# A weight request moved ahead of a small shift in SyncE's queue, and two subtractions moved from GpSimd to VectorE, in a two-layer decoder trunk

## The chip, the cores and the metric

The kernel runs on one core of a Trainium2 chip. The metric is the device time of one execution in microseconds, from which a median over runs is taken. Five engines work side by side, each through its own list of instructions in order: TensorE (PE in the rows, its weight loads PEld), VectorE (DVE), ScalarE (ACT), GpSimd (POOL) and SyncE (SP), which here asks for all DMA transfers.

## What is computed

Two layers over 1024 positions of width 1024: a Mamba-2 mixer, then stick-breaking attention over 16 heads of 64, each followed by a gated per-layer embedding. The change lies in the second layer:

```python
def stick_breaking_mixer(h, k, v, norm_g, w_in, q_g, w_out):
    qg = rmsnorm(h, norm_g) @ w_in
    gate = qg[..., SB_WIDTH:]
    q = rmsnorm(qg[..., :SB_WIDTH].reshape(bsz, s, SB_HEADS, SB_HEAD_DIM), q_g)
    q = (q * (1.0 / math.sqrt(SB_HEAD_DIM))).transpose(0, 2, 1, 3)
    for blk in range(s // SB_BLOCK):
        z = jnp.einsum('bhtd,bhsd->bhts', q[:, :, q0:kend], k[:, :, :kend])
        log_keep = jnp.where(strict, jax.nn.log_sigmoid(-z), 0.0)
        suffix = lax.cumsum(log_keep, axis=3, reverse=True) - log_keep
        weights = jnp.where(strict, jnp.exp(jax.nn.log_sigmoid(z) + suffix), 0.0)
        outs.append(jnp.einsum('bhts,bhsd->bhtd', weights, v[:, :, :kend]))
    return (o * jax.nn.silu(gate)) @ w_out
```

K and V come from the same normalized stream through `w_kv`.

## The kernel before

**Two-part numbers.** Every matrix is split into a high and a low part (`hilo`, L103 to L110): ScalarE writes the high part (L106), then GpSimd or VectorE subtracts it from the raw tile and writes the low part (L108 without a gain, L110 with one, always on VectorE). A product takes three matmuls, high by high, high by low and low by high.

**Pairs and steps.** Attention (`attention`) goes through 8 pairs of heads. A pair has 4 steps, p = 3, 2, 1, 0, each for 256 positions: `project` computes K, Q and V of two blocks (L55), `gate` (in steps p = 1 and 0) half of the pair's gate, `values` shifts V by one row through DMAs and subtracts (L851 to L863), `norm` the rms of K and Q. Work of two earlier steps is mixed in: `flip` transposes K and Q (L883) and splits them into `kst`, `qh` (L894, L895, ScalarE) and `ql` (L898, VectorE); `scores` (L914, L915 on TensorE, a sigmoid L916, a scan L918 on VectorE); `turn` transposes weights and splits them into `wh` (L939, ScalarE) and `wl` (L940, VectorE); `product` multiplies them with V (L948). I call the passage from the last step of one pair to the first of the next a pair change; there are 7.

**The pair's weights.** A pair needs 4 chunks of 512 KB. `Pairs.load` takes one: a DMA into one of three raw tiles (L760, pool `rawp`), then 4 high parts (L106, `g0h`) and 4 low parts (L110, `g0l`). `LOADS` says in which steps p a chunk of the next pair is asked for in the program's text; what is left is taken by `pairs.all` at the start of the pair. Six chunks have room, so four of every pair change are converted while the last gate of the old pair runs and frees their tiles: two of the pair that begins and, after them, two of the pair after it.

**The output weights.** `B2.weights` loads s_out in 8 chunks (L1095, `hh`/`hl`); `CHUNKS` says in which step the first four are asked for. The last four are loaded in step 31, the low parts on GpSimd. `B2.fill` (L1122) multiplies the first two row blocks of the output with them, mixed into the two last rounds of attention; its left-hand sides are split by `B2.ahead` into tiles that are free by then (`V`, `kq`, `vr`, `kst`).

**What sets the order.** TensorE's order is written by hand (`step`). On the other engines and in SyncE's queue a scheduler places the instructions when the program is built, by the order of the text and by estimated times; at run time each engine and each queue takes them strictly in that order, and a waiting one holds all behind it. V's shift has one buffer `vs`: a step's first shift (L853) can only be asked for when GpSimd is done with the one before (L863). In the first step of a pair L853 reads a row of zeros (`vs<-keep`).

Of the kernel before, what the change touches and what calls it, by code (L numbers as in the profile page):

```python
# [28 lines left out]
PLE = 256  # L29
EPS = 1e-6  # L30
ACT_HEADS = (0, 1)
LOADS = (2, 1)
SSB = 1
NEX = 5
EARLY = 3
# [3 lines left out]
GATE7 = {2: 1, 1: 0}  # L39
FLIP = 0.58  # L40
FILL = {32: 7, 33: 6}
CHUNKS = {30: (0, 1, 2, 3)}


def split3(nc, out, pairs):
# [740 lines left out]
def attention(k, A, rawp, hT, oTd, dbg, b2, pairs):  # L786
# [6 lines left out]
    with ExitStack() as ctx:  # L793
# [71 lines left out]
        def norm(st, p):  # L865
            kq = st.pop("kq")
            sq = wk.tile([P, 512], F32, name="sg", bufs=1)
            nc.scalar.activation(sq, kq.rearrange("p b m c -> p (b m c)"), AF.Square)
            n = 8
            ss = sm.tile([P, n], F32, name="kss")  # L870
            nc.vector.reduce_sum(ss, sq.rearrange("p (g d) -> p g d", d=64), axis=AX.X)
            y = k.rstd(sm, ss, n, 64, EPS, "kr")
            x = kq.rearrange("p b m (h d) -> p (b m h) d", d=64)
            nc.vector.tensor_tensor(x, x, y.unsqueeze(2).broadcast_to([P, n, 64]), op=ALU.mult)
            st["kn", p] = kq
# [127 lines left out]
        def step(i):  # L1003
# [34 lines left out]
            if i < n:  # L1038
                if p in LOADS:
                    pairs.step(hp + 1)  # L1040
                values(sts[hp], p)
                norm(sts[hp], p)
                if i in CHUNKS:
                    b2.weights(CHUNKS[i])
                if i == n - 1:
# [19 lines left out]
class B2:  # L1065
# [21 lines left out]
    def weights(self, kks):  # L1087
        k = self.k
        for kk in kks:
            half, i = 1 - kk // 4, kk % 4  # L1090
            if i == 0:
                self.big = [self.hp.tile([P, KT, 512], F32R, name=f"{n}{half}") for n in ("hh", "hl")]
            hi, lo = self.big
            raw = self.rawp.tile([P, 1024], F32, name="raw")
            k.nc.sync.dma_start(raw, self.A["s_out"][kk * P:(kk + 1) * P, :])  # L1095
            sl = slice(2 * i, 2 * i + 2)
            k.hilo(hi[:, sl], lo[:, sl], raw.rearrange("p (n c) -> p n c", n=2))
            self.W[kk] = [(hi[:, 2 * i + n], lo[:, 2 * i + n]) for n in range(2)]

    def ahead(self, t, h, raw, parts):  # L1100
# [190 lines left out]
```

## Time and profile before

| | |
|---|---|
| median of 3 runs | 1876.53 us (1875.95 to 1879.9) |
| the profiled execution | 1882.81 us, span of its instructions 1881.1 us |
| granted TensorE clock, mean over the span | 0.973 |
| TensorE busy | 1737.1 us, 92% |
| VectorE busy | 1177.3 us, 63% |
| ScalarE busy | 901.4 us, 48% |
| GpSimd busy | 412.6 us, 22% |

The profiled execution took 6.3 us more than the median. Busy shares are means over the span; attention runs from about 920 to 1690 us. The granted clock is 1.00 at 2.4 GHz and 0.5 at 1.2 GHz, the two levels that occur.

### The profile page before, as it was taken

Reading aid. Unit: us, or ns where it says so; the run is one execution under the profiler, and the core shown is the slowest. Engines: PE = TensorE matmul, PEld = TensorE weight load, DVE = VectorE, ACT = ScalarE, POOL = GpSimd, SP = SyncE. Lnnn points to the kernel's source line nnn. Section 1 sums busy time; section 2 is a strip of 40 time slices with the busy share of each in tenths; the row PEclk is TensorE's granted clock in tenths of the full one; section 3 lists DMA queues with packets and bytes.
Section 4 is the critical chain, followed back from the end, with each engine's and each line's share of the span. In section 5 each row is a group of like instructions: output and inputs, shape, how many; then the busy total and the mean of one; then the engine's idle time right before and its main releaser. Section 6 shows DMA issues by size and latency. Waiting matters only on the chain.

```text
span 1881.1 us, 25474 instructions
## 1 busy us (share of the span) xinstructions
PE 1737.1 (92%) x9170; PEld 1470.6 (78%) x9170; DVE 1177.3 (63%) x2394; ACT 901.4 (48%) x1976; POOL 412.6 (22%) x454
## 2 busy tenths in 40 slices
PE   7999999999999999999998979888888898689999
PEld 5768877877877877888887968787787888577887
DVE  6686387287278464345668776767676777575332
ACT  6567357358356241134455555555545455453211
POOL 0235534534534122100011101010101013311110
PEclk9999999999999999999998999898989999899999
DMA  4223223223213653322201011010101011223110
GB/s 151 73 71 96 80 72 96 74 68 102 78 63 118 219 175 106 130 95 76 90 19 53 20 48 40 29 53 16 53 16 53 28 30 57 75 90 125 41 51 34
DMA packets 96399, 139.43 MB, mean 74 GB/s; under 512 B 18161, under 2 KB 66641, under 8 KB 96273
## 3 DMA queue, kind: packets, MB, share of 16 engines
q1 hardware_dynamic: 96272, 137.80, 22.7%
q8 instruction: 72, 1.18, 0.3%
q14 instruction: 55, 0.44, 0.1%
HBM read 108.77 MB, written 24.77 MB: 71 GB/s over the span
## 4 chain that ended last, share of the span: by engine, by line
PE 69%; DVE 13%; ACT 8%; DMA 5%; issue 2%; POOL 2%; SPq 0%; DVEq 0%; POOLq 0%; ACTq 0%
PE mm L48 35%; PE mm L55 12%; PE mm L1122 4%; PE oq L948 3%; PE pq L48 2%; DMA vs<-vr 2%; DVE pt L918 2%; DVE v L236 2%; PE intra L411 2%; PE z L915 1%; PE tr L930 1%; PE inter L406 1%; ACT qh L895 1%; PE z L914 1%; ACT qh L894 1%
## 5 line engine op out<-in xcount | busy, mean ns | idle before, releaser
L48 PE MATMUL mm<-ul,wh 128*128 128x512 f32 (+1 forms) x648 | 254.0, 392 | 0.0
L48 PE MATMUL mm<-uh,wl 128*128 128x512 f32 (+1 forms) x648 | 252.5, 390 | 0.0
L48 PE MATMUL mm<-uh,wh 128*128 128x512 f32 (+1 forms) x648 | 252.4, 389 | 0.1
L918 DVE TENSOR_TENSOR_SCAN pt<-pt,keep 128x128 f32<-128x128 f32 (+7 forms) x128 | 173.1, 1357 | 19.0 <-ACT pt L916 17.6
L55 PE MATMUL mm<-g0l,hh 128*128 128x384 f32 x512 | 184.4, 360 | 0.0
L55 PE MATMUL mm<-g0h,hl 128*128 128x384 f32 x512 | 183.5, 358 | 0.0
L55 PE MATMUL mm<-g0h,hh 128*128 128x384 f32 x512 | 181.4, 354 | 0.0
L236 DVE SCALAR_TENSOR_TENSOR v<-u,convh,v 128x512 f32<-128x512 f32 x144 | 128.7, 898 | 55.1 <-ACT v L234 52.6
L939 ACT CAST wh<-tr 128x512 fp32r<-128x512 f32 (+1 forms) x160 | 85.4, 545 | 155.5 <-PE tr L933 147.9
L857 POOL TENSOR_TENSOR vs<-vs,vr 128x256 f32<-128x256 f32 x32 | 24.8, 775 | 598.1 <-DMA vs<-vr 316.1
L940 DVE TENSOR_TENSOR wl<-tr,wh 128x512 fp32r<-128x512 f32 (+1 forms) x160 | 100.7, 634 | 84.2 <-ACT wh L939 83.4
L48 PEld LDWEIGHTS mm<-ul,wh 128*128 128x128 f32 x648 | 121.7, 188 | 26.3 <-issue 2.3
L48 PEld LDWEIGHTS mm<-uh,wl 128*128 128x128 f32 x648 | 121.8, 188 | 25.5 <-issue 1.9
L48 PEld LDWEIGHTS mm<-uh,wh 128*128 128x128 f32 x648 | 121.7, 188 | 25.5 <-issue 1.1
L108 POOL TENSOR_TENSOR wl<-raw,wh 128x1024 fp32r<-128x1024 f32 x39 | 95.2, 2442 | 156.8 <-ACT wh L106 156.8
L916 ACT ACTIVATE pt<-z 128x320 f32<-128x320 f32 (+3 forms) x192 | 94.0, 490 | 67.4 <-PE z L915 66.2
L948 PE MATMUL oq<-wh,V 128*128 128x256 f32 x320 | 65.2, 287 | 46.2 <-issue 34.5
L948 PEld LDWEIGHTS oq<-wh,V 128*128 128x128 f32 x320 | 61.1, 201 | 54.4 <-issue 36.4
L55 PEld LDWEIGHTS mm<-g0l,hh 128*128 128x128 f32 x512 | 101.5, 198 | 2.2
L55 PEld LDWEIGHTS mm<-g0h,hl 128*128 128x128 f32 x512 | 101.1, 198 | 1.6
L55 PEld LDWEIGHTS mm<-g0h,hh 128*128 128x128 f32 x512 | 100.8, 197 | 1.2
L576 DVE SCALAR_TENSOR_TENSOR acc<-mm,rg,acc 128x512 f32<-128x512 f32 x64 | 47.8, 749 | 84.4 <-PE mm L48 83.6
(367 smaller groups left out, 4324.7 us busy)
## 6 DMA issues: line engine op xcount, KB each, us to landing
raw<-in_w_in SPq DMA_DIRECT2D x40, 512.0 KB
ex<-acd SPq DMA_DIRECT2D x64, 256.0 KB
raw<-in_w_b SPq DMA_DIRECT2D x32, 512.0 KB
raw<-in_m_out SPq DMA_DIRECT2D x16, 512.0 KB
raw<-in_gate SPq DMA_DIRECT2D x16, 512.0 KB
graw<-gT SPq DMA_DIRECT2D x30, 256.0 KB
gT<-zs SPq DMA_DIRECT2D x28, 256.0 KB
acc<-in_x SPq DMA_DIRECT2D x8, 512.0 KB
```

Source lines behind the costliest of these rows:

```text
L48: nc.tensor.matmul(out, lhsT=a, rhs=b, start=(i == 0), stop=(i == n - 1))
L55: nc.tensor.matmul(out, lhsT=a, rhs=b, start=(i == 0), stop=(i == n - 1))
L108: (eng or nc.gpsimd).tensor_tensor(lo, raw, hi.bitcast(F32), op=ALU.subtract)
L236: nc.vector.scalar_tensor_tensor(vv, u[:, 3 - j:3 - j + 512], w(j), vv, op0=ALU.mult, op1=ALU.add)
L411: nc.tensor.matmul(aq[hp * 64:hp * 64 + 64, jp * 256 + i * P:jp * 256 + (i + 1) * P], lhsT=xdts[2 * qt + i][:, (2 * j + hp) * 64:(2 * j + ...
L576: nc.vector.scalar_tensor_tensor(acc[:, sl], ps, k.rg[:, g, t:t + 1], acc[:, sl], op0=ALU.mult, op1=ALU.add)
L916: nc.scalar.activation(pt[:, ko:ko + n], z[:, :n], AF.Sigmoid, scale=-1.0)
L918: nc.vector.tensor_tensor_scan(pt[:, :N], pt[:, :N], keep[:, :N], 1.0, op0=ALU.mult, op1=ALU.max)
L939: nc.scalar.copy(wh[:, :c], tq[:, :c])
L940: nc.vector.tensor_tensor(wl[:, :c], tq[:, :c], wh[:, :c].bitcast(F32), op=ALU.subtract)
L948: nc.tensor.matmul(out[:, :w], lhsT=st["V"][j // 2][:, j % 2, h * P:(h + 1) * P], rhs=rhs, start=(j0 == 2 * p and i == 0), stop=(j0 == NT ...
L1122: nc.tensor.matmul(pss[n], lhsT=a, rhs=b, start=(q == 0 and i == 0), stop=(q == 1 and i == 11))
```

## The change

Three tables and one argument. `LOADS` now asks for a chunk of the next pair in each of the four steps, so nothing is left for `pairs.all`; `CHUNKS` asks for the first two s_out chunks in step 29, not 30; and the low parts of s_out chunks 5 and 7 are computed on VectorE.

```diff
-LOADS = (2, 1)
+LOADS = (3, 2, 1, 0)
...
-CHUNKS = {30: (0, 1, 2, 3)}
+CHUNKS = {29: (0, 1), 30: (2, 3)}
...
-            k.hilo(hi[:, sl], lo[:, sl], raw.rearrange("p (n c) -> p n c", n=2))
+            k.hilo(hi[:, sl], lo[:, sl], raw.rearrange("p (n c) -> p n c", n=2), eng=k.nc.vector if kk in (5, 7) else None)
```

What that does to the order, at the three places that matter. SyncE's queue at a pair change, before (L851 is the large shift of V, 127 rows, L853 and L852 are one-row shifts, L856 copies a row, L760 is a chunk of weights):

```order
L851 DMA vs<-vr 127x256
L856 DMA v_9882<-vr 128x1x1
L853 DMA vs<-keep 1x16x8
L760 DMA raw<-in_w_b 128x1024 x4
L852 DMA vs<-vr 1x16x8
```

and the same place now:

```order
L851 DMA vs<-vr 127x256
L856 DMA v_9910<-vr 128x1x1
L760 DMA raw<-in_w_b 128x1024
L853 DMA vs<-keep 1x16x8
L760 DMA raw<-in_w_b 128x1024 x3
L852 DMA vs<-vr 1x16x8
```

One chunk has moved ahead of the shift of zeros. This is so at five pair changes, from pair 1 to 2 up to pair 5 to 6; at the one from pair 6 to 7 the chunk is one of s_out. At the one from pair 0 to 1 a chunk stood ahead of L853 before already, and still does.

ScalarE at the same pair change, before:

```order
L894 CAST qh<-tr 64x256
L895 CAST qh<-tr 64x256
L829 COPY kq<-mm 128x256
L830 COPY vr<-mm 128x128
L959 COPY of<-oq 64x256
L106 ACTIVATE g0h<-raw,kvn 128x256
L916 ACTIVATE pt<-z 128x320
L106 ACTIVATE g0h<-raw,sn 128x256
```

and now:

```order
L894 CAST qh<-tr 64x256
L106 ACTIVATE g0h<-raw,kvn 128x256
L106 ACTIVATE g0h<-raw,sn 128x256
L895 CAST qh<-tr 64x256
L829 COPY kq<-mm 128x256
L830 COPY vr<-mm 128x128
L959 COPY of<-oq 64x256
L916 ACTIVATE pt<-z 128x320
```

Two conversions of weights have moved ahead of the last `qh` copy and of the copies of K, Q and V. This is so at six pair changes, from pair 1 to 2 up to pair 6 to 7. On VectorE the fourth low part (L110) of the first chunk has moved ahead of a 640 wide scan there.

GpSimd in the last steps of attention, as a piece of the difference (`hl` are low parts of s_out, chunk 4 above, 5 to 7 below in the old order; `V<-raw` is the low part of the left-hand side that the first `fill` needs):

```order
 L863 TENSOR_TENSOR V<-vs,V 128x128 x2
+L108 TENSOR_TENSOR V<-raw,V 128x512
 L108 TENSOR_TENSOR hl_15604<-raw,hh_15603 128x1024
-L108 TENSOR_TENSOR V<-raw,V 128x512
-L108 TENSOR_TENSOR hl_15604<-raw,hh_15603 128x1024 x2
 L108 TENSOR_TENSOR kst<-raw,kst 128x896
```

Chunk 5's low part no longer stands ahead of `V<-raw`, and chunk 7's no longer ahead of `kst`. On VectorE they now stand inside the chain of small operations of the last `norm`, and between two `wl`. TensorE's order is the same.

## Rows read from the trace of the kernel before

**Rows 1.** The page, part 4: the chain that ended last, by engine.

```profile
PE 69%; DVE 13%; ACT 8%; DMA 5%; issue 2%; POOL 2%; SPq 0%; DVEq 0%; POOLq 0%; ACTq 0%
```

**Rows 2.** Timeline of TensorE at pair changes: start, us, operation [idle before <-releaser].

```profile
1090.10 0.66 PE L948 MATMUL oq<-wh,V 128*128 128x256 f32 x2 [6.72 <-issue]
...
1180.75 0.69 PE L948 MATMUL oq<-wl,V 128*128 128x256 f32 x2 [0.67 <-DVE wl L940]
...
1456.11 0.66 PE L948 MATMUL oq<-wh,V 128*128 128x256 f32 x2 [6.64 <-issue]
```

**Rows 3.** The chain that ended last, pair 2 to 3: start, us, what.

```profile
1160.15 7.91 DMA vs<-vr
...
1169.90 1.03 POOL V L863 x2
...
1170.95 0.56 SPq L853
...
1171.55 3.86 DMA raw<-in_w_b
```

**Rows 4.** Timeline, ScalarE, pair 2 to 3.

```profile
1175.50 0.51 ACT L106 ACTIVATE g0h<-raw,kvn 128x256 fp32r<-128x256 f32 x1 [7.36 <-DMA raw<-in_w_b]
```

**Rows 5.** Timeline, VectorE, pair 2 to 3.

```profile
1176.04 0.48 DVE L110 SCALAR_TENSOR_TENSOR g0l<-raw,kvn,g0h 128x256 fp32r<-128x256 f32 x1 [3.30 <-ACT g0h L106]
1177.30 0.69 DVE L844 TENSOR_TENSOR GT<-mm,sg 128x512 f32<-128x512 f32 x1 [0.77 <-ACT sg L843]
```

**Rows 6.** Busy time by stretch: its length, PE, PEld, DVE, ACT, POOL, PEclk, DMA.

```profile
1066.97:1091.43 24.46, 16.27 (x94) 14.23 (x92) 18.07 (x31) 16.12 (x40) 4.47 (x10) 0.94 0.21 70
1156.39:1180.75 24.36, 16.26 (x94) 14.23 (x92) 18.07 (x31) 16.12 (x40) 4.45 (x10) 0.93 0.21 71
977.17:998.70 21.53, 17.54 (x94) 15.37 (x92) 18.21 (x31) 17.45 (x43) 4.29 (x10) 0.92 0.24 80
1523.99:1541.95 17.96, 15.94 (x93) 14.10 (x91) 15.72 (x26) 13.18 (x32) 5.07 (x10) 1.00 0.09 19
1180.75:1186.52 5.77, 5.29 (x25) 4.87 (x26) 5.08 (x20) 1.60 (x4) 0.00 (x0) 0.72 0.29 90
998.70:1006.04 7.34, 5.40 (x26) 4.98 (x26) 6.66 (x24) 2.44 (x7) 0.00 (x0) 0.77 0.37 102
982.50:986.00 3.50, 3.50 (x12) 2.95 (x11) 3.41 (x7) 2.62 (x7) 0.00 (x0) 0.51 0.06 16
1179.42:1184.00 4.58, 3.91 (x14) 3.63 (x15) 4.11 (x14) 1.35 (x3) 0.00 (x0) 0.51 0.00 0
```

**Rows 7.** Timeline, pair 0 to 1: ScalarE, SyncE's queue and TensorE.

```profile
980.39 0.49 ACT L106 ACTIVATE g0h<-raw,sn 128x256 fp32r<-128x256 f32 x1
...
991.21 0.51 ACT L106 ACTIVATE g0h<-raw,kvn 128x256 fp32r<-128x256 f32 x1 [0.31 <-DMA raw<-in_w_b]
...
984.31 0.36 SPq L760 DMA_DIRECT2D raw<-in_w_b  x1
...
981.64 0.41 PE L915 MATMUL z<-kst,ql 128*128 128x320 f32 x1 [1.61 <-DVE ql L898]
```

**Rows 8.** Timeline, TensorE, pair 2 to 3.

```profile
1160.06 0.41 PE L915 MATMUL z<-kst,ql 128*128 128x320 f32 x1 [0.81 <-DVE ql L898]
```

**Rows 9.** Timeline of the last steps: TensorE, GpSimd, VectorE.

```profile
1638.88 1.22 PE L1122 MATMUL mm<-hh,V 128*128 128x512 f32 x2 [9.89 <-POOL V L108]
...
1635.26 2.34 POOL L108 TENSOR_TENSOR hl<-raw,hh 128x1024 fp32r<-128x1024 f32 x1
...
1642.14 0.56 DVE L940 TENSOR_TENSOR wl<-tr,wh 128x384 fp32r<-128x384 f32 x1 [12.10 <-ACT wh L939]
```

**Rows 10.** L108 by shape: count, ns min/median/max, first and last start.

```profile
L108 DVE TENSOR_TENSOR wl<-raw,wh x1: 1226/1226/1226, 15.3 to 15.3; 128x1024 fp32r<-128x1024 f32 x1
...
L108 POOL TENSOR_TENSOR ol<-raw,oh x6: 2116/2120/2584, 1704.7 to 1822.6; 128x896 fp32r<-128x896 f32 x6
...
L108 POOL TENSOR_TENSOR kst<-raw,kst x1: 5420/5420/5420, 1663.3 to 1663.3; 128x896 fp32r<-128x896 f32 x1
```

## The prediction

> **What bounds the kernel now.** I read the chain that ended last first: TensorE carries 69% of it, VectorE 13%, ScalarE 8%, transfers 5% [rows 1]. So the change is worth what it takes from TensorE's waits, and the next view is TensorE's timeline, searched for waits above 0.6 us in attention. At five pair changes, from pair 1 to 2 up to pair 5 to 6, it stands still for 6.62 to 6.72 us ahead of a product with `wh`, and 0.67 us more for `wl` (first and last of the five, and one of the second kind) [rows 2]. Five times 7.3 us is 37 us in the reach of this change; at the change from pair 0 to 1 and from 6 to 7 no such wait stands.
>
> The chain of pair 2 to 3 tells where it comes from [rows 3]: V's large shift is asked for at 1160.15 and takes 7.91 us, GpSimd makes V from it until 1170.93, only then does SyncE ask for the shift of zeros (L853), since `vs` has one buffer, and behind that, at 1171.55, for the fourth chunk of weights, which lands 3.86 us later. ScalarE, in order, stands 7.36 us at that chunk's first conversion [rows 4]. TensorE does not need the chunk for a whole pair; it needs what is queued behind it on ScalarE: the sigmoid, `sg`, `wh`. VectorE stands too, 3.30 us for the chunk and 0.77 us for `sg`, and then works on without a pause until the `wl` that TensorE waits for [rows 5].
>
> **The change part by part.**
>
> *One chunk ahead of L853, five times.* It needs a raw tile, and the raw tile is free when VectorE has done the first chunk's fourth low part. The pair change from 0 to 1 has had the new order all along and serves as the measured case. There the chunk was asked for at 984.31, 7.1 us after that change's `flip` transposes (977.17), and ScalarE had it at 991.21, 6.9 us after the request [rows 7]. Put on pair 2 to 3, with `flip` at 1156.39, that is a request at 1163.5 and a landing at 1170.4, instead of 1175.4. VectorE finishes its scan at 1172.74 (1176.04 less its 3.30 idle) [rows 5], so the chunk is there before VectorE wants it. What is late next is VectorE itself: the gate product, a 768 wide scan, a sum and `wl` follow without a gap, so TensorE's product moves forward by at most VectorE's two idle times, 3.30 + 0.77 = 4.07 us. That is the upper end. The lower end is the measured case as it stands: from `flip` to the first `wl` product it took 21.53 us, the five others 24.36 to 24.46 (two of them shown) [rows 6]. 24.4 - 21.5 = 2.9 us. Nothing of the 7.3 us beyond 4.07 is to be had, since VectorE's work there, 18.07 us in the 24.36, stays [rows 6].
>
> *Two conversions ahead of the last `qh` copy on ScalarE, six times.* They are 0.49 us each, a little overlapped (980.39 is one of the measured case's) [rows 7], and hold `ql`, and with it the scores' second matmul. In the measured case TensorE waited 1.61 us for it [rows 7], in pair 2 to 3 only 0.81 [rows 8]: the price is 0.8 us for TensorE, of which VectorE, which paces the rest, feels at most as much. Behind the copies of K, Q and V queue the big shift and then L853, all 0.8 us later; V from them is first multiplied two steps later (`product` works on `steps[i - 2]`), and that covers it. In the measured case the granted clock was 0.51, the lower level, for the 3.50 us from 982.50, right after the 1.61 us wait [rows 6]; in pair 2 to 3 it stayed at the upper level there. That half speed costs up to 1.7 us, and is inside the 21.53.
>
> Between 2.9 and 4.07 I take 3.2 us for each of the five: the measured case has the same order on all engines and the same wait, so it is the nearest row; a little is added because the fall of the clock that it holds need not come each time. 5 x 3.2 = 16.0 us. The sixth place, pair 6 to 7, has the conversions ahead of `qh` but no wait to lose (17.96 us in the same stretch, clock 1.00) [rows 6]: it costs between 0.4 and 0.8 + 1.7 = 2.5 us; I take 0.8, the wait alone.
>
> *After the wait.* TensorE's clock is at 0.51 for 4.58 us once it resumes [rows 6]. I count no gain there: the measured case, whose remaining waits are short, shows 0.77 over the 7.34 us that follow, beside 0.72 over 5.77 us [rows 6].
>
> *The low parts of s_out.* TensorE waits 9.89 us, until 1638.88, for the low part `V<-raw`, which stands on GpSimd behind chunk 5's low part of 2.34 us [rows 9]. With that gone it starts 2.3 us earlier. On VectorE the part costs 1.226 us (the one of its shape) [rows 10], inside 12.10 us in which VectorE waits for `wh` [rows 9]: nothing. Chunk 7's part stands between two `wl`; both wait for TensorE then, so I cost it at nothing, at most 1.2 us if its high part is late. The s_out chunks that are asked for earlier are converted at the same place of ScalarE's order as before: nothing. Gain 2.3, bounds 1.1 and 2.4.
>
> One rule speaks against the move. A GpSimd subtraction of 128x896 took 5.42 us in these last steps, six others of that shape 2.12 in the median [rows 10]. The Trainium skill, SBUF — State Buffer, section Who interferes with whom, says that a VectorE instruction with two SBUF inputs and a GpSimd instruction that reads SBUF exclude each other for the whole instruction; the moved parts are of that kind. The slowed row is in line with it. By that rule chunk 7's part could hold GpSimd's chunk 6, and it would take at most its 1.2 us back. Chunk 5's meets no GpSimd work, which is waiting for V's shift then.
>
> Sum: 16.0 + 2.3 - 0.8 = 17.5 us. The profiled execution, 1882.81 us, would take 1865.3. It was 6.3 us above the median, of which nothing is tied to this place, so I take the same 17.5 off the median: **1859.0 us**.
>
> **The rivals.**
>
> *The next stretch takes it back* (VectorE and the clock become the bound). For: the measured case needs 7.34 us from the first `wl` product to the next `flip`, where pair 2 to 3 needs 5.77, so that from `flip` to `flip` it gains only 28.87 against 30.13: 1.3 us [rows 6]. Against: it converts a fifth chunk in that stretch, which the five others don't. Time: 5 x 1.3 + 2.3 - 0.8 = 8.0, 1868.5 us.
>
> *The clock holds.* With the long wait gone the slow stretch of 4.58 us behind it might go too; that is half of it, 2.2 us, in each of the five, 11 us more: 1848 us [rows 6]. The Trainium skill, TensorE: Matmul & The Clock Gate, section What's actually happening, has activity release a throttle and idleness restore it, which is for this rival. Against it stands the measured case: clock 0.51 after a wait of 1.61 us only.
>
> *It doesn't do what it says:* the chunk waits for its raw tile as long as for the shift, and only the 2.3 us at the end come: 1874 us. Against: the request at 984.31 [rows 7].
>
> *Slower.* ScalarE's new order costs 0.8 us and a slow stretch of 1.7 at six places, 15 us, and the request buys nothing, because the chunk, now on the way beside the large shift, lands no earlier than ScalarE reaches it now. It decides at 1175.4, 11.9 us after the request; the measured landing was 6.9. 1876.5 + 15 - 2.3 = 1889 us.
>
> **How the numbers follow.** Forecast 0.62; taken back 0.17; clock holds 0.08; nothing but the end 0.08; slower 0.05. The unknown costs alone give 5 x 4.07 + 2.4 - 0.4 = 22.4 and 5 x 2.9 + 1.1 - 2.5 = 13.1, that is 1854 to 1863; slow stretches may come or go elsewhere in attention by 1.7 us apiece, and the range reaches to the first two rivals: 1849 to 1869 us. Faster by over 0.2% (3.8 us, about what a measurement of this kernel can tell from no change): 0.62 + 0.17 + 0.08 = 0.87; within it 0.08; slower 0.05.
>
> **What would show it.** Right: at five pair changes SyncE asks for one chunk some 7 us after `flip`, ahead of L853, ScalarE's wait of 7.36 is gone or below 1 us, TensorE's wait ahead of the `wh` product is 2 to 4 us, VectorE has no idle time above 1 us between the last conversions and `wl`, and from `flip` to `wl` it takes 20.4 to 21.6 us. TensorE's wait for `ql` is 1.6 us at six places. At the end the wait for `V<-raw` is 2.3 us shorter. Wrong: a landing more than 9 us after the request; a wait of TensorE for `of`, V or `wl` later in the pair that is longer than before; stretches from `flip` to `flip` that shrink by less than 2 us.

## The result and the profile after

The changed kernel takes **1851.22 us** in the median of 4 runs (1848.77 to 1852.96); the kernel before, in runs on the same chip, 1878.22 us (1875.95 to 1881.54, also 4). The ratio is 0.9854 with a 95% interval from 0.9833 to 0.9875: 27.0 us less, where the prediction said 17.5. The profiled execution took 1852.96 us (span 1851.2).

The chain that ended last, by engine, of the changed kernel; it answers to [rows 1]:

```profile
PE 74%; DVE 14%; ACT 7%; DMA 2%; issue 2%; POOL 1%; SPq 0%; DVEq 0%; POOLq 0%; ACTq 0%
```

Transfers have gone from 5% to 2%, and TensorE's share has grown from 69% to 74%. The timeline of the change from pair 2 to 3 in the changed kernel, by engine (start, us, engine, line, operation, in brackets the idle time before it and what ended it); it answers to [rows 2 to 5, 8]:

```profile
1158.44 0.41 PE L915 MATMUL z<-kst,ql 128*128 128x320 f32 x1 [1.61 <-DVE ql L898]
1172.51 0.41 PE L948 MATMUL oq<-wh,V 128*128 128x256 f32 x2 [1.32 <-issue]
...
1161.05 0.35 SPq L760 DMA_DIRECT2D raw<-in_w_b  x1
1170.40 0.56 SPq L853 DMA_DIRECT2D vs<-keep  x1
...
1168.00 0.51 ACT L106 ACTIVATE g0h<-raw,kvn 128x256 fp32r<-128x256 f32 x1 [1.86 <-DMA raw<-in_w_b]
...
1168.37 1.75 DVE L918 TENSOR_TENSOR_SCAN pt<-pt,keep 128x640 f32<-128x640 f32 x1
1170.04 0.61 DVE L110 SCALAR_TENSOR_TENSOR g0l<-raw,kvn,g0h 128x256 fp32r<-128x256 f32 x1
1170.68 0.69 DVE L844 TENSOR_TENSOR GT<-mm,sg 128x512 f32<-128x512 f32 x1
1173.53 0.55 DVE L940 TENSOR_TENSOR wl<-tr,wh 128x384 fp32r<-128x384 f32 x1
1176.90 0.56 DVE L940 TENSOR_TENSOR wl<-tr,wh 128x384 fp32r<-128x384 f32 x1
```

The first `flip` transpose of this change stands at 1153.97. SyncE asks for the fourth chunk at 1161.05, 7.1 us later, and for the shift of zeros (L853) only at 1170.40: the chunk is no longer behind it. It lands 6.9 us after the request; ScalarE still waits for it, 1.86 us instead of 7.36. VectorE's rows are the ones to read closely: the scan at 1168.37, the low part at 1170.04, the gate product at 1170.68 and `wl` carry no bracket. The 3.30 and 0.77 us of [rows 5] are both gone. TensorE waits 1.32 + 1.22 us for `wh` and `wl` instead of 6.62 + 0.67, and 1.61 instead of 0.81 for `ql`.

Busy time by stretch in the changed kernel (length, PE, PEld, DVE, ACT, POOL, granted clock, DMA share, GB/s), as in [rows 6]: from `flip` to the first `wl` product in the changes of pair 2 to 3, 0 to 1 and 6 to 7; then from `wl` to the next `flip` in the changes of pair 2 to 3 and 1 to 2:

```profile
1153.97:1174.14 20.17, 16.02 (x94) 14.11 (x92) 17.62 (x31) 16.34 (x40) 5.29 (x10) 1.00 0.19 60
977.95:999.48 21.53, 17.58 (x94) 15.47 (x92) 18.04 (x31) 17.22 (x43) 4.25 (x10) 0.92 0.24 80
1495.62:1514.02 18.40, 15.80 (x94) 14.17 (x92) 15.85 (x26) 13.39 (x32) 4.52 (x10) 1.00 0.15 48
...
1174.14:1179.41 5.27, 5.27 (x25) 4.97 (x26) 4.92 (x19) 1.21 (x4) 0.00 (x0) 0.68 0.53 187
1087.98:1093.17 5.19, 3.86 (x25) 3.50 (x26) 4.99 (x20) 1.61 (x4) 0.00 (x0) 1.00 0.50 176
```

24.4 us have become 20.15 (20.10 to 20.22 at the five), and 5.77 have become 5.27. From `flip` to `flip` the five pair changes take 25.39 us in the mean (25.30 to 25.46), before 30.33 (30.13 to 30.94): 4.94 us each, 24.7 in all. Pair 6 to 7 takes 22.45 instead of 22.02, 0.43 us more. At the end, from pair 6 to 7's second `flip` to the end of the span, it is 333.2 instead of 335.1 us. 24.7 - 0.4 + 1.9 = 26.2 us of the 27.0. The last term is good to about a us only: with the same code there, a second execution of the changed kernel took 333.6 us, and the order of loads alone, an edit that doesn't touch the end, 336.2 where before has 335.1.

The last steps of the changed kernel (TensorE, VectorE, GpSimd), as in [rows 9] and [rows 10]:

```profile
1608.99 0.80 PE L1122 MATMUL mm<-hh,V 128*128 128x512 f32 x1 [7.54 <-POOL V L108]
...
1600.51 1.23 DVE L108 TENSOR_TENSOR hl<-raw,hh 128x1024 fp32r<-128x1024 f32 x1
1613.71 1.23 DVE L108 TENSOR_TENSOR hl<-raw,hh 128x1024 fp32r<-128x1024 f32 x1 [0.90 <-ACT hh L106]
...
1633.41 5.42 POOL L108 TENSOR_TENSOR kst<-raw,kst 128x896 fp32r<-128x896 f32 x1 [20.08 <-ACT kst L106]
```

The wait for `V<-raw` is 7.54 us instead of 9.89. The two moved low parts take 1.23 us each on VectorE, as the one of their shape in [rows 10], and `kst` takes the 5.42 us that it took before.

### The profile page after: what moved, and what is told of

Same layout as the page of the kernel before. It is cut to its first block, busy times and chain, and to the rows that moved or that the text cites. A ratio compares the mean times of both kernels' runs of the same rounds, so it can differ in the third digit from the quotient of the medians.

```text
span 1851.2 us, 25501 instructions
## 1 busy us (share of the span) xinstructions
PE 1731.0 (94%) x9170; PEld 1465.7 (79%) x9170; DVE 1173.9 (63%) x2396; ACT 903.0 (49%) x1976; POOL 413.2 (22%) x452
## 4 chain that ended last, share of the span: by engine, by line
PE 74%; DVE 14%; ACT 7%; DMA 2%; issue 2%; POOL 1%; SPq 0%; DVEq 0%; POOLq 0%; ACTq 0%
PE mm L48 36%; PE mm L55 14%; PE mm L1122 5%; PE oq L948 3%; PE pq L48 2%; DVE pt L918 2%; PE z L915 2%; DVE v L236 2%; PE intra L411 2%; PE z L914 1%; PE tr L930 1%; PE inter L406 1%; ACT qh L895 1%; PE tr L666 1%; ACT qh L894 1%
## 5 line engine op out<-in xcount | busy, mean ns | idle before, releaser
L918 DVE TENSOR_TENSOR_SCAN pt<-pt,keep 128x128 f32<-128x128 f32 (+7 forms) x128 | 174.0, 1364 | 21.9 <-ACT pt L916 20.6
L857 POOL TENSOR_TENSOR vs<-vs,vr 128x256 f32<-128x256 f32 x32 | 24.1, 754 | 567.4 <-DMA vs<-vr 489.9
L108 POOL TENSOR_TENSOR wl<-raw,wh 128x1024 fp32r<-128x1024 f32 x39 | 95.2, 2441 | 156.7 <-ACT wh L106 156.7
L649 DVE SCALAR_TENSOR_TENSOR pth<-pth,pq 128x512 f32<-128x512 f32 (+1 forms) x33 | 22.2, 671 | 104.9 <-PE pq L48 100.2
L373 ACT ACTIVATE ex<-ex,acum 128x128 f32<-128x128 f32 x256 | 86.5, 389 | 0.8
```

The lines of the kernel that those rows point to most:

```text
L108: (eng or nc.gpsimd).tensor_tensor(lo, raw, hi.bitcast(F32), op=ALU.subtract)
L373: nc.scalar.activation(x, x, AF.Relu, bias=acum[:, c:c + 1])
L918: nc.vector.tensor_tensor_scan(pt[:, :N], pt[:, :N], keep[:, :N], 1.0, op0=ALU.mult, op1=ALU.max)
```

## The experiments

Each ran beside executions of the kernel before on the same chip; ratios are against those, with 95% intervals. Two executions of one kernel can differ by several us in places that no edit touches (last section), so beside the ratio each verdict rests on a passage or a wait in the trace.

### Which part of the change pays

The order of loads alone, on the kernel before:

```diff
-LOADS = (2, 1)
+LOADS = (3, 2, 1, 0)
```

> The kernel before with LOADS = (3, 2, 1, 0) alone; the chunks of s_out and the low parts as before. Theory A (the time of one request is what the change is worth): from flip to the next flip the five pair changes take 25.3 to 25.5 us as in the changed kernel, instead of 30.1 to 30.9; from pair 6 to 7 the passage takes 0.4 us more than before; at the end the wait for the low part of V stays at 9.9 us. Gain 5 x 4.9 - 0.4 = 24 us, ratio about 0.987. Rival B (a good part of the 27 us came from the end of attention or from clock luck elsewhere): the five passages shrink by 3.2 us or less each, gain 16 us or less, ratio 0.9915 or more.

1850.86 us, ratio 0.9852 [0.9826, 0.9878]. The five changes take 25.35 to 25.55 us from `flip` to `flip`, as in the changed kernel. Pairs 0 to 1 and 2 to 3 from `flip` to `wl` in this kernel (columns as above):

```profile
975.66:995.88 20.22, 16.02 (x93) 14.11 (x92) 17.67 (x31) 15.86 (x39) 5.32 (x10) 0.99 0.19 60
1149.02:1169.17 20.15, 16.02 (x94) 14.11 (x92) 17.60 (x31) 16.34 (x40) 5.29 (x10) 1.00 0.19 60
```

And its TensorE's timeline at the end:

```profile
1605.75 0.80 PE L1122 MATMUL mm<-hh,V 128*128 128x512 f32 x1 [9.85 <-POOL V L108]
```

The one request carries nearly all of the gain, and the wait for `V<-raw` stays at 9.85. The first of the two stretches surprised me: pair 0 to 1, whose order this edit leaves alone, takes 20.22 us at clock 0.99, not the 21.53 at 0.92 that the prediction used.

The two low parts alone:

```diff
-            k.hilo(hi[:, sl], lo[:, sl], raw.rearrange("p (n c) -> p n c", n=2))
+            k.hilo(hi[:, sl], lo[:, sl], raw.rearrange("p (n c) -> p n c", n=2), eng=k.nc.vector if kk in (5, 7) else None)
```

> The kernel before with the two low parts (chunks 5 and 7 of s_out) on VectorE alone. Theory: TensorE's wait for the low part of V falls from 9.89 to 7.5 us, pair changes as before, gain 2.3 us, ratio 0.9988. Rival (VectorE's part holds GpSimd's): GpSimd's part of chunk 4 or 6 takes over 3 us instead of 2.34 and the gain is 1.1 or less. The whole time alone cannot tell these apart; the waits can.

1876.62 us, ratio 0.9993 [0.9977, 1.0009]: too little to be seen in the time. TensorE's timeline of this kernel at the end:

```profile
1630.19 0.79 PE L1122 MATMUL mm<-hh,V 128*128 128x512 f32 x1 [7.55 <-POOL V L108]
```

And its pair 0 to 1 from `flip` to `wl`:

```profile
978.25:998.47 20.22, 16.02 (x93) 14.11 (x91) 17.67 (x31) 15.86 (x39) 5.33 (x10) 1.00 0.19 58
```

The wait at the end is shorter by 2.34 us, the end of the span comes 1.7 us sooner after the last counted `flip` (333.4 against 335.1), and the five pair changes are as before (30.05 to 30.31 us). This kernel has the order of before at every pair change, and its pair 0 to 1 takes 20.22 us: the case that the prediction measured was an execution that happened to be slow at this place.

### What the request gains by: the shift of zeros, or its place

Two other ways of getting the chunk sooner, with the order of LOADS left as before. A second buffer for `vs`, so that L853 needn't wait for GpSimd (paid for by one buffer of `of`):

```diff
-            vs = wk.tile([P, 2, P], F32, name="vs", bufs=1)
+            vs = wk.tile([P, 2, P], F32, name="vs", bufs=2)
...
-                st["of"] = wk.tile([P, 256], F32, name="of", bufs=2)
+                st["of"] = wk.tile([P, 256], F32, name="of", bufs=1)
```

> The kernel before with two buffers for vs (and one for of, to make room); LOADS as before, so the order on ScalarE, VectorE and GpSimd is that of before, and SyncE still has the shift of zeros (L853) ahead of the chunk. Theory A (the chunk was late because L853 waited for vs, nothing else): L853 is asked for at once, the chunk some 7 us after flip, ScalarE's wait of 7.36 us goes, and from flip to the first wl product the five pair changes take 20 to 20.5 us instead of 24.4, the same as with the new order. As the two conversions stand behind the qh copies, TensorE waits 0.81 us for ql and not 1.61, pair 6 to 7 pays nothing, and at pair 0 to 1 the fall of the clock after the 1.61 us wait does not come (21.53 becomes about 20). Gain 5 x 4.5 to 5 x 5 and 1.4: 24 to 26 us, ratio 0.986 to 0.987. Rival C (the order of the conversions is part of the gain): the five passages stay 0.4 to 0.8 us longer than in the changed kernel, gain 19 to 22 us. Rival D (the raw tile, not vs, holds the request): no gain, ratio 1.000.

1850.83 us, ratio 0.985 [0.9825, 0.9876]. The timeline of pair 2 to 3 in this kernel, `flip` at 1152.36, for SyncE, ScalarE and TensorE:

```profile
1157.81 0.67 SPq L853 DMA_DIRECT2D vs<-keep  x1
1160.61 0.34 SPq L760 DMA_DIRECT2D raw<-in_w_b  x1
...
1165.53 0.51 ACT L106 ACTIVATE g0h<-raw,kvn 128x256 fp32r<-128x256 f32 x1 [1.42 <-DMA raw<-in_w_b]
...
1156.04 0.42 PE L915 MATMUL z<-kst,ql 128*128 128x320 f32 x1 [0.81 <-DVE ql L898]
1170.93 0.41 PE L948 MATMUL oq<-wh,V 128*128 128x256 f32 x2 [2.16 <-issue]
```

Its stretch there from `flip` to `wl`, and 4.50 us of pair 0 to 1 behind the wait for `ql`:

```profile
1152.36:1172.56 20.20, 16.02 (x94) 14.02 (x92) 17.95 (x31) 16.24 (x40) 4.23 (x10) 1.00 0.30 86
980.79:985.29 4.50, 4.50 (x16) 3.89 (x16) 4.37 (x8) 3.61 (x9) 0.00 (x0) 0.62 0.05 13
```

Here L853 does stand ahead of the request, but it goes out at once, and the chunk is asked for 8.25 us after `flip`. The stretch takes 20.20 us at all five changes. The rivals fell that wanted the order of ScalarE's conversions for the gain: TensorE waits 0.8 us less for `ql` here, and 0.84 more for `wh`. Where I was wrong: I expected this kernel to lose the wait for `ql` in pair 0 to 1 too; that place had the new order all along, and kept the wait and, this time, the slow clock behind it.

The big shift cut into 112 and 15 rows, on the kernel before:

```diff
-            nc.sync.dma_start(vs[0:P - 1], vr[1:P])
+            _ = [nc.sync.dma_start(vs[a:b], vr[a + 1:b + 1]) for a, b in ((0, 112), (112, P - 1))]
```

> The kernel before with V's large shift (L851) as two transfers, 112 and 15 rows, instead of one of 127; SyncE still asks for the shift of zeros ahead of the chunk. The 127 KB of that shift took 7.91 us where the 512 KB of a chunk took 3.86. Theory G (the shift is the first link of the wait: it is slow because of its 127 rows, and nothing but its end holds the request): the two parts land in 3 to 4.5 us, GpSimd has V 3 to 4 us earlier, the shift of zeros and the chunk are asked for 3 to 4 us earlier, and from flip to the first wl product the five pair changes take 20.2 to 21.5 us with the request still behind the shift. Gain 15 to 24 us, ratio 0.987 to 0.992. Rival H (a move inside SBUF takes that long in any shape, or waits for the same engines): the parts land as late, the additional issue of 0.6 us makes it 0.5 us later, ratio 1.000 to 1.002. The Trainium skill, DMA: Bandwidth & Descriptors, section Why a DMA increments its semaphore by 16 and not by 1, has 127 partitions carried by a single DMA engine and 112 by sixteen; by that Theory G holds.

1849.61 us, ratio 0.9849 [0.9822, 0.9876]. The transfers' view of this kernel (destination and source, queue, count, KB each, median us to landing):

```profile
vs<-vr SPq DMA_DIRECT2D x32, 112.0 KB, 2.1
vs<-vr SPq DMA_DIRECT2D x32, 15.0 KB, 2.0
```

Its pair 2 to 3 from `flip` to `wl`:

```profile
1150.78:1171.10 20.32, 16.05 (x93) 14.04 (x91) 18.07 (x31) 16.25 (x40) 3.74 (x5) 1.00 0.27 85
```

And the timeline there, SyncE and ScalarE:

```profile
1159.46 0.35 SPq L760 DMA_DIRECT2D raw<-in_w_b  x1
1161.25 0.54 SPq L853 DMA_DIRECT2D vs<-keep  x1
...
1163.08 0.51 ACT L106 ACTIVATE g0h<-raw,kvn 128x256 fp32r<-128x256 f32 x1 [0.54 <-DMA raw<-in_w_b]
```

The shift lands in 2.1 us where one transfer of 127 rows took 7.91 [rows 3]. The Trainium skill, DMA: Bandwidth & Descriptors, section Why a DMA increments its semaphore by 16 and not by 1, says that 127 partitions put everything on one engine, and that a count that sixteen divides spreads over sixteen. Both landings agree with it. The expectation took the request to follow the shift of zeros; it went out ahead of it, 8.7 us after `flip`, since the scheduler's order moved. So this run doesn't separate the shift's length from the request's place; it shows a third way to the same 20.3 us. At the end it takes 333.3 us, 1.8 less than before without any moved low part.

All three ways end within 20.1 to 20.3 us. They don't add up, either: the second buffer on top of the changed kernel, and the cut shift on top of it (each with the edit shown above):

> The changed kernel with two buffers for vs (one for of): the new order on ScalarE and VectorE, but SyncE has the shift of zeros, which no longer waits, ahead of all four chunks. Theory: nothing is left to gain from the request, 20.1 to 20.2 us from flip to the first wl product at the five pair changes, the wait for ql stays 1.61 us and with it the clock falls at none to two of the seven places; 1849 to 1852 us. Rival: the two ways add, and the passages fall below 20 us.

1850.05 us, ratio 0.9848 [0.9823, 0.9873]: 20.12 to 20.35 us at the pair changes but for one of 21.52 with a fall of the clock.

> The changed kernel with the same two transfers for V's large shift. The chunk is asked for ahead of the shift of zeros already, so theory: nothing more to gain between flip and wl, 20.1 to 20.3 us at the five pair changes, 1848 to 1852 us; GpSimd's work on V comes 3 to 4 us earlier, beside other instructions of VectorE, and may cost or give 0.5 us there. Rival: the chunk's own landing (6.9 us after its request) was long because the shift was on the way beside it; then it lands in 4 to 5 us, which VectorE, busy until then, doesn't notice either. Only a gain over 5 us would say that something else than VectorE sets the passage.

1849.76 us, ratio 0.9849 [0.9823, 0.9875]. From `flip` (1153.13) to `wl` in pair 2 to 3 it takes 20.61 us, 0.45 more than in the changed kernel, though ScalarE waits for no transfer any more. This kernel's stretch:

```profile
1153.13:1173.74 20.61, 16.02 (x93) 14.10 (x92) 18.05 (x31) 16.25 (x40) 4.13 (x5) 1.00 0.26 84
```

And GpSimd and VectorE in its timeline there:

```profile
1162.51 0.85 POOL L857 TENSOR_TENSOR vs<-vs,vr 128x256 f32<-128x256 f32 x1 [12.67 <-PE mm L55]
...
1162.68 0.96 DVE L110 SCALAR_TENSOR_TENSOR g0l<-raw,sn,g0h 128x256 fp32r<-128x256 f32 x1
```

V comes sooner, and so GpSimd's sum for it now falls on VectorE's conversions: one L110 takes 0.96 us instead of 0.48, VectorE's busy time is 18.05 instead of 17.62, and the whole difference is in it. The end of the span comes 2.7 us sooner after the last `flip` (330.5 against 333.2), and five times 0.45, with three falls of the clock (last part of this section), takes that back.

### Is VectorE the bound now

If VectorE's chain sets `wl`, a cut of its work must show. In the changed kernel the low parts of one chunk are made for 128 of 256 columns only, with zeros from GpSimd in the other half (q is the chunk). Two chunks were tried, in two kernels, q == 2 and q == 3:

```diff
-                    k.hilo(hi[:, sl], lo[:, sl], raw[:, i * 512 + m * 256:i * 512 + m * 256 + 256], gain=g)
+                    k.nc.scalar.activation(hi[:, sl], raw[:, i * 512 + m * 256:i * 512 + m * 256 + 256], AF.Copy, scale=g); w = 128 if hp >= 2 and q == 2 else 256; k.nc.vector.scalar_tensor_tensor(lo[:, m * 256:m * 256 + w], raw[:, i * 512 + m * 256:i * 512 + m * 256 + w], g, hi[:, m * 256:m * 256 + w].bitcast(F32), op0=ALU.mult, op1=ALU.subtract); w < 256 and k.nc.gpsimd.memset(lo[:, m * 256 + 128:m * 256 + 256].bitcast(F32), 0.0)
```

> The changed kernel with less work on VectorE at the pair changes: of the first converted chunk (q = 2, pairs 2 to 7) the four low parts are made for 128 of their 256 columns, the other columns are set to zero on GpSimd (that part of the computation is left out). The order on every engine stays. Each part becomes 0.13 to 0.2 us shorter (0.48 us for 128x256, 0.25 for 128x128), 0.6 us in all. Theory (after the change VectorE, which goes without a pause from ql to wl, sets the pair change): from flip to the first wl product 20.15 becomes 19.4 to 19.7 us at the five pair changes. Rival (ScalarE's conversions or the landing of the fourth chunk set it): it stays at 20.1 to 20.2 and VectorE gets an idle time of 0.6 us instead.

1849.62 us, ratio 0.985 [0.983, 0.987]. The stretch stayed at 20.03 to 20.22 us: not what was expected. Pair 2 to 3 of this kernel, `flip` at 1150.85, on VectorE:

```profile
1157.02 0.35 DVE L768 SCALAR_TENSOR_TENSOR g0l<-raw,kvn,g0h 128x128 fp32r<-128x128 f32 x1 [0.28 <-ACT g0h L768]
1157.74 1.49 DVE L918 TENSOR_TENSOR_SCAN pt<-pt,keep 128x640 f32<-128x640 f32 x1
```

The cut instructions come so early that VectorE then waits for ScalarE's high part. The scan behind them starts 6.89 us after `flip`, in the changed kernel 6.96: what was cut was taken up at once by ScalarE, and the run says nothing on the rest of the chain. So the other chunk, whose low parts are later:

> The changed kernel with the four low parts of the second converted chunk (q = 3, pairs 2 to 7) made for 128 of 256 columns, the rest set to zero on GpSimd (that part of the computation is left out); the order on the engines stays. With the first chunk's parts halved nothing was gained: VectorE waited 0.28 us for ScalarE's third high part there, and the scan after it began at 6.89 us after flip instead of 6.96. Behind that scan VectorE goes without a pause to wl. Theory (from there VectorE alone sets the pair change): the four parts end 0.4 to 0.6 us earlier and everything behind them too, from flip to the first wl product 19.6 to 19.75 us instead of 20.15 at the five pair changes. Rival (ScalarE's conversions or sg set it at every point): again 20.1 to 20.2.

1850.34 us, ratio 0.9851 [0.9822, 0.988]. Two of the five changes now take 19.70 us, and pair 6 to 7 takes 17.65 instead of 18.40; the three others take 20.20 to 20.24. In this kernel, pair 3 to 4 and pair 5 to 6 from `flip` to `wl`:

```profile
1237.86:1258.10 20.24, 16.01 (x93) 14.10 (x91) 17.69 (x31) 16.34 (x40) 5.77 (x14) 1.00 0.19 60
1407.64:1427.34 19.70, 16.03 (x94) 14.12 (x92) 17.14 (x31) 16.27 (x40) 5.99 (x14) 1.00 0.15 47
```

VectorE and GpSimd in the timeline of each:

```profile
1250.69 1.03 DVE L768 SCALAR_TENSOR_TENSOR g0l<-raw,sn,g0h 128x256 fp32r<-128x256 f32 x1
1250.70 0.74 POOL L857 TENSOR_TENSOR vs<-vs,vr 128x256 f32<-128x256 f32 x1 [10.92 <-DVE of L960]
...
1420.49 0.48 DVE L768 SCALAR_TENSOR_TENSOR g0l<-raw,sn,g0h 128x256 fp32r<-128x256 f32 x1
1420.65 0.91 POOL L857 TENSOR_TENSOR vs<-vs,vr 128x256 f32<-128x256 f32 x1 [11.18 <-DVE of L960]
```

Where VectorE kept its cut, `wl` came half a us sooner: VectorE's chain does set it. In the three others VectorE was 0.5 us ahead until the two engines met: low part and sum start within 0.03 us of each other there, GpSimd's sum takes the 0.74 us that it takes alone, and the low part 0.99 to 1.03 us for 0.48. In the two that gained VectorE was first by 0.10 and 0.16 us, kept its 0.48, and GpSimd took 0.98 and 0.91 instead of 0.74.

### GpSimd's long subtraction, and what else the end holds

The 128x896 low part of `kst`, cut in three, in the changed kernel:

```diff
-                tail[n + 1] = ahead(FILL[n + 1], [(kt[:, 0, :7], kt[:, 1, :7], 0, 7)])
+                tail[n + 1] = ahead(FILL[n + 1], [(kt[:, 0, a:b], kt[:, 1, a:b], a, b - a) for a, b in ((0, 2), (2, 4), (4, 7))])
```

> The changed kernel with the split of kst at the end of attention in three pieces (2, 2 and 3 blocks) instead of one of 7, on ScalarE and GpSimd. TensorE waits 4.70 us there for GpSimd's 5.42 us. Theory E (the part is slow all along, since VectorE works on two operands in SBUF beside it): the first piece is done after 2/7 of it, 1.6 us, the wait falls to 1 to 1.5 us, and the time is 3 to 3.5 us below the changed kernel's. Rival F (the part stands still first, while VectorE's scan of 2.28 us runs, and goes fast later): the first piece alone takes 3 us or more and the gain is 1.5 us or less. Beside the kernel before: 0.984 or 0.985.

1848.64 us, ratio 0.9845 [0.9813, 0.9877]. GpSimd, VectorE and TensorE in this kernel's timeline:

```profile
1629.16 4.61 POOL L108 TENSOR_TENSOR kst<-raw,kst 128x256 fp32r<-128x256 f32 x1 [19.45 <-ACT kst L106]
...
1630.98 2.28 DVE L918 TENSOR_TENSOR_SCAN pt<-pt,keep 128x1024 f32<-128x1024 f32 x1
1633.18 0.66 DVE L1127 TENSOR_TENSOR GT<-mm,GT 128x512 f32<-128x512 f32 x1
...
1633.83 0.50 PE L1122 MATMUL mm<-hh,kst 128*128 128x512 f32 x1 [3.33 <-POOL kst L108]
```

The first piece, 128x256, took 4.61 us; the same shape takes 0.74 at 1585.7 in this kernel (`kq<-raw`), beside VectorE's L898 and L960, which have one input from a matmul's result. VectorE ran two-input instructions without a gap until then, the last a scan of 2.28 us, and the piece ends 0.6 us after VectorE turned to L1127, one of whose inputs is a matmul's result. So most of the 5.42 us are, by these rows, time in which GpSimd was held off, as the rival had it, and smaller pieces help only in that the first of them releases TensorE (3.33 us of wait instead of 4.70).

The best of all this together: the second `vs` buffer, the two low parts and the three pieces on the kernel before; and the same with V's low part on VectorE and chunk 7's back on GpSimd:

```diff
-            k.hilo(hi, lo, raw[:, k0:k0 + m])
+            k.hilo(hi, lo, raw[:, k0:k0 + m], eng=nc.vector if (t, k0) == (FILL[32], 0) else None)
```

> The kernel before with two buffers for vs (one for of), the two low parts of s_out on VectorE and kst in three pieces; LOADS and CHUNKS as before. Theory: the parts add. Two buffers gave 1850.8 us; the low parts take 2.0 to 2.3 us off TensorE's wait for V (9.85 to 7.55) and the split of kst 1.3 us (4.70 to 3.33): 1847 to 1848 us, ratio 0.9835. Rival: the gains at the end run into a later wait (the last row block's low part, 1.4 to 1.7 us) and 1850 us stand.

> As the kernel with two buffers for vs, the low parts and the split of kst, but at the end the low part of V is made on VectorE, which waits 8.7 us there, and chunk 7's low part goes back to GpSimd. Theory: VectorE makes V's low part right after ScalarE's high part, TensorE's wait of 7.55 us shrinks to 1.5 us or less; what is then late is the s_out chunk that lands last (ScalarE converts it at 1612.6 in the changed kernel, 3.6 us after that wait ends), so only 1 to 2.5 us of the 6 come out at the end: 1845 to 1847 us. Rival: chunk 7's low part, now 2.4 us on GpSimd instead of 1.2 on VectorE, is what the last product waits for, and nothing is gained: 1847 to 1849.

1847.99 us, ratio 0.9836 [0.9814, 0.9858], and 1848.35 us, ratio 0.9837 [0.9818, 0.9857]. TensorE's timeline of the second:

```profile
1601.61 0.80 PE L1122 MATMUL mm<-hh,V 128*128 128x512 f32 x1 [1.02 <-DVE V L108]
...
1611.73 0.47 PE L883 MATMUL tr<-ident,kq 128*128 128x128 f32 x1 [4.29 <-DVE wl L940]
```

The wait for `V<-raw` falls from 7.55 to 1.02 us, and part of it comes back ten us later: TensorE waits 4.29 us for `wl` there, in the first kernel 1.53. From the last counted `flip` (pair 6 to 7's second) to the end it is 330.6 us against 332.3 in the first and 333.2 in the changed kernel.

The changed kernel once more, beside these two:

> The changed kernel itself once more, beside the others on one chip. 1850 to 1853 us. In its trace: at the five pair changes 20.1 to 20.2 us from flip to the first wl product, unless the clock falls after the wait of 1.61 us for ql (then 21.5); that fall stood at pair 0 to 1 in three of six executions so far and at two of eighteen other places, so at zero to three of the seven places here.

1849.46 us, ratio 0.9851 [0.983, 0.9872]: some 1.3 us more than the two, well within the intervals. The runs don't show that either beats it; the traces have the end alone shorter, by 0.9 to 3.0 us, and an end differs by about a us between executions of the same code. In this execution the five pair changes take 20.1 to 20.25 us from `flip` to `wl`, about as expected, and the clock falls at two of the seven places, pair 0 to 1 and 6 to 7; the time is half a us below what was expected. (In the six traces at hand when the expectation was written there were three falls at the eighteen other places, not two.)

### The clock behind a short wait

The prediction's measured case had a wait of 1.61 us for `ql` with the granted clock at its lower level behind it. Pair 0 to 1 and pair 2 to 3 of the changed kernel, 4.50 us each from the end of that wait:

```profile
982.42:986.92 4.50, 4.50 (x16) 3.95 (x17) 4.41 (x9) 3.38 (x9) 0.00 (x0) 0.63 0.06 13
1158.44:1162.94 4.50, 4.50 (x24) 3.98 (x25) 4.42 (x9) 4.13 (x12) 0.00 (x0) 1.00 0.08 18
```

In pair 0 to 1 of its second execution, just above, it is 0.65. A mean of 0.62 to 0.65 is most of the stretch at 1.2 GHz, 16 matmul rows instead of 24; 1.00 is 2.4 GHz throughout. Counted so over the traces of before, after and all twelve runs: 12 falls behind 62 waits of 1.61 us, none behind 36 waits of 0.81 us. The same place falls in one execution and not in the next (pair 0 to 1 falls in before, after, after again and the second `vs` buffer on before; in the ten others it doesn't). In the changed kernel, TensorE's instructions ahead of the wait stand within 0.1 us of each other in pairs 0 to 1 (fall) and 1 to 2 (none). So the fall is chance, about one in five here, and with it the stretch from `flip` to `wl` takes 21.5 instead of 20.15 us, 1.35 more, in seven of the twelve places; at pair 6 to 7, and where the shift is cut in the changed kernel, it is about 0.6 more. The Trainium skill, TensorE: Matmul & The Clock Gate, section What's actually happening, has the activity monitor run freely, so that the same kernel shows different clocks from run to run: these counts agree.

## Why the prediction was right in its mechanism and short in its size

**What bounded the kernel: right.** The chunk was late because its request stood behind L853. Taking the request out of there gains all of it, by any of three ways.

**What is late next: right.** VectorE has no idle time left from the landing to `wl`; half a us off VectorE's late low parts brings `wl` half a us sooner where GpSimd leaves it alone.

**"Between 2.9 and 4.07 I take 3.2": wrong, the step that failed.** The value between the two ends was taken by the wrong row, and even the upper end was passed by 0.1 us. The pair change from 0 to 1 had the right order of instructions, but its 21.53 us held a fall of the clock, and I allowed for it only "a little". Without a fall the same place takes 20.2 us (20.20 to 20.35 in the eight runs without it and with the shift whole). 24.4 - 20.2 = 4.2 us is the term. VectorE's two idle times, 4.07 us, were much the better price. The gate product stood 20.91 us behind `flip` and stands 16.71 behind it now, 4.20 sooner, and `wl` moved by 4.19. That the sum comes so near is in part chance, since three more terms nearly cancel. These are rows of the kernel before in pair 2 to 3:

```profile
1159.59 0.88 DVE L898 TENSOR_TENSOR ql<-tr,qh 64x256 fp32r<-64x256 f32 x2 [0.54 <-ACT qh L895]
1161.94 0.49 DVE L110 SCALAR_TENSOR_TENSOR g0l<-raw,sn,g0h 128x256 fp32r<-128x256 f32 x1 [0.38 <-ACT g0h L106]
```

`ql` began 3.20 us behind `flip` on VectorE and begins 4.00 behind it now (1157.97), so VectorE loses the 0.80 us of the conversions in full; the idle 0.38 us ahead of a low part is gone as well; and VectorE's busy time is 17.62 instead of 18.07 us, in part since its instructions meet GpSimd's less (one L110 had taken 0.97 us there, now none takes over 0.61). 5 x (4.2 - 3.2) = 5 us of the missing 9.5.

**"I count no gain there" (after the wait): wrong, 0.5 us at four places, 1.3 at the fifth.** From `wl` to `flip` it took 5.77 and takes 5.27 us. The granted clock there is as low as before (0.68 against 0.72) at four of the five, and at the fifth, pair 1 to 2, where it stays at 1.00, the stretch takes 5.19 us, hardly less: this is not the clock coming back. In the kernel before, VectorE's next `wl` waited 0.49 us for a `wh`, as this row of its timeline shows, in the 4.58 us at clock 0.51 right behind the long wait [rows 6]; in the changed kernel the one at 1176.90 (first block) follows without a wait:

```profile
1184.01 0.56 DVE L940 TENSOR_TENSOR wl<-tr,wh 128x384 fp32r<-128x384 f32 x1 [0.49 <-ACT wh L939]
```

The 0.49 us are measured; their cause is argued: VectorE had nothing left to do while TensorE caught up, and now it arrives later relative to TensorE and finds `wh` made. The measured case of 7.34 us in [rows 6] could not show this, since it converts a fifth chunk there. In the mean over the five it is 5.93 against 5.25 us, 3.4 us in all (0.8 of them from one place of the kernel before, pair 3 to 4, with 6.57 us at clock 0.52): with the 5 above, 8.4 of the missing 9.5; the rest is smaller than the interval.

**The sixth place, forecast -0.8: measured -0.43.** The wait for `ql` came as told, 1.61 us at all six; of the 0.8 more, half reached `wl` (18.40 against 17.96 us). With a fall of the clock behind it (this kernel's second profile has one, 19.0 us instead of 18.40) it is about -1.0.

**The end, forecast 2.3: measured 1.9 (1.7 with the low parts alone), good to about a us.** The step was right: the wait itself is 2.35 us shorter in the changed kernel and 2.34 with the low parts alone. Of the rule that speaks against it nothing came, since neither moved part met work of GpSimd; `kst` is as long as before.

**The rivals.** *The next stretch takes it back* fell: that stretch got shorter. *The clock holds* named 1848 us, and the time came out near it, but not by its mechanism: the stretch behind the `wh` product still runs at 0.67 to 0.68 at four of the five places, and at the fifth, at 1.00, it is no more than 0.1 us shorter. *It doesn't do what it says* and *slower* fell with the request 7.1 us behind `flip` and the landing 6.9 later.

**The signs.** Three were missed. ScalarE's wait was to be below 1 us and is 1.86; VectorE, not ScalarE, paces there, so it costs nothing. TensorE's wait ahead of the `wh` product was to be 2 to 4 us and is 1.26 to 1.40. The stretch was to be 20.4 to 21.6 us and is 20.15, from the failed step.

**Range and chances.** 1851.2 lies in 1849 to 1869, near its lower edge. It is below the 1854 us that the bounds of the unknown costs allowed (the two idle times in full, 22.4 us off), since the 0.5 us a place behind the wait were in no bound. It lies in the range only because that had been widened for other reasons (slow stretches elsewhere, the rivals): that part was luck.

## What to carry to other kernels

Before a measured case is used as the price of a move, read its clock: a case that holds a slow stretch is an upper bound on the time, and a second execution or a sister place without the slow stretch gives the price. When a wait disappears, sum the idle times of the engine that paces next; that sum was within 0.13 us here (with three smaller terms that nearly cancelled), and the neighbouring case was 1.3 us off. A request that stands behind another wait on a queue can be freed from either side (its place, the buffer that blocks the one in front, the transfer before it), and doing two of these brought nothing more here.

## What the runs showed that I had not expected

- **A short wait of TensorE can cost more than itself.** 1.61 us of idle time was followed by the lower clock in 12 of 62 places, 0.81 us in none of 36, at 0.6 to 1.35 us a fall. Where two orders differ by 0.8 us in such a wait, the shorter has by these counts an expected gain of at most 12/62 x 1.35 = 0.26 us on top.
- **VectorE and GpSimd hold each other up, both ways.** GpSimd's 128x256 took 4.61 us instead of 0.74 beside VectorE's L110 and scan; VectorE's L110 took 1.03 and 0.96 instead of 0.48 where L857 was running. The Trainium skill, SBUF — State Buffer, section Who interferes with whom, says that they share one pair of ports as an exclusive lock. The rows are in line with it, though the delays are somewhat shorter than the other's whole instruction. Which of the two kept its length went by who was first in the five pair changes with the half low parts: VectorE did where it led by 0.10 and 0.16 us.
- **A profiled execution differs from the next by up to 8 us in places that no edit touched.** In attention, passages come in two lengths some 1.6 us apart (21.9 or 23.46, 19.07 or 20.66 us) in most runs, the short ones at clock 1.00 and the long ones at 0.86 to 0.93 in the traces of before, after and the low parts alone, so the long ones hold falls of the clock: from the first to the last counted `flip` the kernel before took 568.84 us with 7 long ones of 18, the one with the low parts alone, which has the same code there, 560.83 with 3. A term of 2 us is to be read from its own passage, not from two spans.
